# A transformer encoder in one kernel: the order of a gate and up group, and which PSUM pool its accumulators and the attention's transposes use

## The chip, the cores and the metric

The kernel runs on one core of a Trainium2 chip. The metric is device time in microseconds (us), from the first to the last instruction of one launch. The engines named below are TensorE (PE, matrix products, with its weight loads PEld), VectorE (DVE), ScalarE (ACT), GpSimd (POOL) and SyncE (SP, which issues the transfers). Each executes its own list of instructions in the order in which the list was written when the kernel was built.

## The reference

One sequence of 256 tokens with 2048 channels passes two layers and a final norm, all in float32:

```python
h = x + concat(attn, conv, sgu) @ w_out      # all three read RMSNorm(x) @ w_in
x = h + (silu(n @ w_gate) * (n @ w_up)) @ w_down     # n = RMSNorm(h), D_FF = 5632
# attn: 8 query heads on 2 key/value heads of 128, window +-128, a sink logit
#   per head in the softmax, rotary on the first 32 of 128 channels
# conv: GLU, depthwise convolution of width 31, LayerNorm, silu
# sgu:  gelu, LayerNorm of one half, mixing of positions, product with the other half
```

## The kernel before

**Numbers.** The activations are held transposed, as 16 tiles of 128 channels by 256 tokens (`xs`). Every float32 operand is split into a high part and a rest, and each product is three matmuls (xh wh, xh wl, xl wh). Weights are streamed by SP in chunks of 1 MB (`raw`), three at a time. ACT casts half a chunk to its high part (`wh`, L136) and DVE subtracts it (`wl`, L137), four units ahead of PE.

**Stages of a layer.** `proj` (L494) makes the four convolution inputs, two key heads, the values, eight query heads (four pairs p), then the v and u halves of the gating unit. For each query pair: two projections, a copy to `qT` by ACT, the rotary step on DVE (`rope`: a shuffle, two products, a sum, L524 to L529), scores for two token tiles (`pS`, two matmuls each, L536), the softmax on DVE and ACT (scaling and mask L541, maximum L546, exponentials L549, reciprocal L554, scaling L556), and for the pair before, `mix_values` (L561): four transposes of the probabilities into `pT`, a copy `pts` by ACT, the products `po` with the values, and the split of the result into `mix`. The depthwise convolution is 31 steps for each of four channel tiles on DVE (L602), given a low priority so that a scheduler spreads it between other work; its norm (`conv_norm`) is taken up in steps between later work.

**Output projection, then feed-forward.** `feed_sums` (L317) transposes each finished column group of the residual on PE (`pt`, L294), scales it on ACT (`xg`), splits it, and prepares sums and differences (`gf`, `gh`, `gd`). After each group the ACT squares it for the norm (`TokenSums.add`, L346). The feed-forward runs in 11 groups of 512 columns. One group (`gate_up`, L418) walks over eight pairs of 128-channel tiles: a pair of kind P takes eight plain products into the accumulators m2, m3, m4, m5; a pair of kind S takes seven products (a Strassen-like form) into m1 to m7. At its end ACT copies and DVE sums turn the seven accumulators into gate and up.

**PSUM.** There are three pools of buffers: `ps` with tag ps (5), `pm` with tag pm (2) and `pm` with tag pmc (1). All projection accumulators (acc, acct, ao, ad) are in ps. Before, m1, m7, m6, m2, m3 are in ps, m5 in pmc, m4 in pm, and pS, pT, po, pt share pm.

**Order.** The program is written in the order above. A scheduler with a model of the engines then decides the place of each instruction on its engine; a pool gives a buffer to its users in the order of the program, and a later user waits until the earlier one has been read. The chip executes the result without any further choice.

Of the kernel before, what the change touches and what calls it, by code (L numbers as in the profile page):

```python
# [10 lines left out]
F32 = mybir.dt.float32  # L11
# [6 lines left out]
P = 128  # L18
D = 2048
S = 256  # L20
# [19 lines left out]
G = 512  # L40
# [8 lines left out]

UP_PAIRS = [(4, "P"), (5, "S"), (6, "P"), (7, "S"), (0, "P"), (1, "S"), (2, "P"), (3, "P")]  # L50
KIND = dict(UP_PAIRS)
LAST_S = max(i for i, (_, kind) in enumerate(UP_PAIRS) if kind == "S")

PARTS = [(0, 3), (3, 3), (6, 3), (9, 2)]

# [104 lines left out]
def chunk_kinds():  # L160
    kinds = []
    for _ in range(DEPTH):
        kinds += ["P"] * (MIX_COLS * KT // CH + D * KT // CH)
        for _, gn in PARTS:
            kinds += [kind for _, kind in UP_PAIRS] * gn
            kinds += ["P"] * (4 * gn * D // CH)
    return kinds

# [2 lines left out]
def encoder_kernel(  # L171
# [19 lines left out]
    ps = ctx.enter_context(tc.tile_pool(name="ps", bufs=5, space=PSUM))  # L191
# [223 lines left out]
        c = slice(t * P, (t + 1) * P)  # L415
        return xs_part(k, 0)[:, c], xs_part(k, 1)[:, c]

    def gate_up(forms, pending):  # L418

        plan = []
        for i, kind in UP_PAIRS:
            if kind == "S":
                order = [
                    (1, x_form(2 * i, 0)), (2, x_form(2 * i + 1, 0)), (3, forms[i][3]),  # L430
                    (7, forms[i][2]), (5, forms[i][0]), (6, forms[i][1]),
                    (4, x_form(2 * i + 1, 1)),
                ]
                plan.append([(m, x, 0) for m, x in order])
            else:
                one = []
                for j in range(2):
                    x1, x2 = x_form(2 * i + j, 0), x_form(2 * i + j, 1)
                    one += [(2, x1, 0), (3, forms[i][j], 1), (5, x2, 2), (4, x2, 3)]
                plan.append(one)  # L440
        seq = [m for block in plan for m, _, _ in block]
        left = {m: seq.count(m) for m in set(seq)}
        bank = {}
        for m in (1, 7, 6, 2, 3):
            bank[m] = ps.tile([P, G], F32, tag="ps", name=f"m{m}")
        bank[5] = pm.tile([P, G], F32, tag="pmc", name="m5", bufs=1)
        bank[4] = pm.tile([P, G], F32, tag="pm", name="m4", bufs=2)
        begun = set()

        def product(m, x, wh, wl):  # L450
            left[m] -= 1
            three_tok(bank[m], x[0], x[1], wh, wl, m not in begun, left[m] == 0)
            begun.add(m)

        s1, u2, u3 = unit("s1")[:, :G], unit("u2")[:, :G], unit("u3")[:, :G]
        for b, block in enumerate(plan):
            if b == 1 and pending:
                hidden_parts(*pending)
            if UP_PAIRS[b][1] == "S":
                for m, x, _ in block:  # L460
                    product(m, x, *W.take(G))
            else:
                for j in range(2):
                    gh, gl = W.take(G)
                    uh, ul = W.take(G)
                    for m, x, q in block[4 * j:4 * j + 4]:
                        if q in (0, 3):
                            product(m, x, gh, gl)
                        else:
                            product(m, x, uh, ul)  # L470
            if b == LAST_S:
                nc.scalar.copy(out=s1, in_=bank[1])
                nc.vector.tensor_tensor(out=u2, in0=bank[6], in1=s1, op=ALU.add)
                nc.vector.tensor_tensor(out=u3, in0=bank[7], in1=u2, op=ALU.add)
        s3, c22 = unit("s3")[:, :G], unit("c22")[:, :G]
        nc.vector.tensor_tensor(out=s1, in0=bank[2], in1=s1, op=ALU.add)
        nc.scalar.copy(out=s3, in_=bank[3])
        nc.vector.tensor_tensor(out=s3, in0=bank[5], in1=s3, op=ALU.add)
        sub(c22, bank[5], u3)
        nc.vector.tensor_tensor(out=u3, in0=bank[4], in1=u3, op=ALU.add)  # L480
        sub(s3, s3, u2)
        return (s1, u3), (s3, c22)
# [77 lines left out]

    def mix_values(p, t, sm, v):  # L561
        g = p // 2
        pT = pm.tile([P, 4, P], F32, tag="pm", name="pT")
        for hh in range(2):
            for kt in range(2):
                nc.tensor.transpose(
                    pT[:, 2 * hh + kt, :], sm[:, hh, kt * P:(kt + 1) * P], ident
                )
        pts = unit("pts")[:, :4 * P].rearrange("p (a b) -> p a b", a=4)
        nc.scalar.copy(out=pts, in_=pT)  # L570
        po = pm.tile([P, 4, P], F32, tag="pm", name="po")
        for hh in range(2):
            for kt in range(2):
                nc.tensor.matmul(
                    po[:, hh, :], v[:, kt, g * P:(g + 1) * P], pts[:, 2 * hh + kt, :],
                    start=(kt == 0), stop=(kt == 1),
                )
        hilo(
            hm[p][:, :, t * P:(t + 1) * P], hm[p][:, :, S + t * P:S + (t + 1) * P], po[:, :2, :]
        )  # L580
# [103 lines left out]
    sums = Sums("in", nc.gpsimd)  # L684
# [6 lines left out]
    for l in range(DEPTH):  # L691
# [81 lines left out]
        for n, kts, begin, end, complete in OUT_ORDER:  # L773
            if begin:
                accs[n] = token_acc("ao")
            for i, k in enumerate(kts):
                wh, wl = W.take(G)
                token_products(
                    [accs[n]], lambda p: hm_part(k, p), wh, wl,
                    begin == 1 and i == 0, end == 1 and i == len(kts) - 1,  # L780
                )
            if end:
                add_residual(n, accs.pop(n))
            next(cnorm, None)
            if complete:
                feed_sums(n, C_G2 + l * KT, forms)
                sums.add(n)


        rf = sums.rstd(f"b{l}")  # L790
        last_layer = l == DEPTH - 1
        if last_layer:
            gf = consts.tile([P, D], F32, tag="lr", name="gf")
            nc.sync.dma_start(gf, lrow[DEPTH])
        sums = TokenSums(f"n{l}")
        pending = None

        def hidden_parts(ht, i0):
# [4 lines left out]

        for g0, gn in PARTS:
            for j in range(gn):
                gate, up = gate_up(forms, pending)
                if j == 0:
                    new_hm(2 * gn, f"h{l}_{g0}_")
                for t in range(2):
                    nc.scalar.activation(gate[t], gate[t], AF.Silu, scale=rf[:, t:t + 1])  # L810
                    nc.vector.scalar_tensor_tensor(
                        out=up[t], in0=up[t], scalar=rf[:, t:t + 1], in1=gate[t],
                        op0=ALU.mult, op1=ALU.mult,
                    )
                ht = up
                pending = (ht, 4 * j)
            end = g0 + gn == FF // G
            for n in range(NG):
                acc = token_acc("ad")
                for i in range(4 * gn):  # L820
                    if n == 0 and i == 4 * (gn - 1):
                        hidden_parts(*pending)
                        pending = None
                    wh, wl = W.take(G)
                    token_products(
                        [acc], lambda p: hm_part(i, p), wh, wl, i == 0, i == 4 * gn - 1
                    )
                add_residual(n, acc)
                if end:
                    sums.add(n)  # L830
                    if not last_layer:
                        feed_group(n, C_G1 + (l + 1) * KT)
                    elif n < NG - 1:
                        f = slice(n * G, (n + 1) * G)
                        for t in range(2):
                            nc.vector.tensor_tensor(
                                out=xt[t][:, f], in0=xt[t][:, f], in1=gf[:, f], op=ALU.mult
                            )
# [22 lines left out]
def _pack_weights(w_in, w_out, w_gate, w_up, w_down):  # L861
# [17 lines left out]
    for l in range(DEPTH):  # L879
# [18 lines left out]
        for g0, gn in PARTS:  # L898
            for j in range(g0, g0 + gn):
                c = slice(j * G, (j + 1) * G)  # L900
                gu = np.concatenate([w_gate[l][:, c], w_up[l][:, c]], axis=1)
                for i, kind in UP_PAIRS:
                    pair = (2 * i, 2 * i + 1)
                    if kind == "S":
                        put(gu, pair, G, G)
                        put(gu, pair, 0, G)
                    else:
                        put(gu, pair, 0, 2 * G)
            for n in range(NG):
                put(w_down[l], range(4 * g0, 4 * (g0 + gn)), n * G, G)  # L910
# [67 lines left out]
```

## Time and profile before

| | us |
|---|---|
| median of 3 runs | 2006.45 (2006.19 to 2008.48) |
| the profiled execution | 2005.52, span 2003.7 |
| PE busy | 1972.7 (98%), mean granted clock 0.996 |
| DVE busy | 1560.8 (78%) |
| ACT busy | 1060.5 (53%) |
| POOL busy | 27.8 (1%) |
| transfers | 381 MB, mean 190 GB/s |

The span runs from the first to the last instruction. PE is busy in 98% of it, and the chain of work that ended last consists of PE for 97%. A row of the timeline has its start, its duration, the engine, the line, the operation, out<-in, shapes, the count, and in brackets the idle time before it and what ended it. Matmuls overlap in the pipeline, so the cost of one is the distance between starts. PEclk is the clock that PE was granted, as a share of 2.4 GHz.

### The profile page before, as it was taken

The numbers are of one execution on the slowest core, as the hardware profiler recorded it, in microseconds if no ns is written. First come the engines' busy times: TensorE is split into PE (matmuls) and PEld (weight loads), VectorE is DVE, ScalarE is ACT, GpSimd is POOL, SyncE is SP. The second block draws the span as 40 slices with busy tenths as digits, with TensorE's granted clock in tenths as the row PEclk, the third lists the DMA queues.
The fourth block names the chain that finished last, engine by engine and source line by source line (L and its number), as shares of the span: only waits on it lengthen the run. The fifth ranks groups of instructions, "written<-read, shape, count | busy, mean of one in ns | idle before, by whom it ended". The sixth has DMA issues, their size and how long they took to land.

```text
span 2003.7 us, 25514 instructions
## 1 busy us (share of the span) xinstructions
PE 1972.7 (98%) x9998; PEld 1682.5 (84%) x9998; DVE 1560.8 (78%) x1984; ACT 1060.5 (53%) x1367; POOL 27.8 (1%) x49
## 2 busy tenths in 40 slices
PE   8999999999999999999999999999999999999997
PEld 8998887888888888888899888788888888888886
DVE  8997679866886788578679975898678857885784
ACT  6456556544554455445543565656445545554553
POOL 3000000000000000000000000000000000000000
PEclk9999999999999999999999999999999999999999
DMA  7554544555555455545555445355555655555552
GB/s 288 193 187 148 210 162 179 192 214 184 191 201 210 176 202 214 191 184 215 184 176 183 155 145 204 128 210 190 210 184 196 224 192 172 212 205 189 197 203 105
DMA packets 55705, 380.96 MB, mean 190 GB/s; under 512 B 6304, under 2 KB 8608, under 8 KB 10272
## 3 DMA queue, kind: packets, MB, share of 16 engines
q1 hardware_dynamic: 55584, 379.33, 52.5%
q8 instruction: 78, 1.28, 0.3%
q14 instruction: 43, 0.35, 0.0%
HBM read 377.21 MB, written 2.10 MB: 189 GB/s over the span
## 4 chain that ended last, share of the span: by engine, by line
PE 97%; ACT 1%; DVE 1%; DMA 0%; issue 0%; SPq 0%; POOLq 0%; DVEq 0%
PE m L410 15%; PE m L411 15%; PE m L412 15%; PE ad L411 8%; PE ad L412 8%; PE ad L410 8%; PE acc L394 4%; PE acc L395 4%; PE acc L396 4%; PE ao L410 3%; PE ao L411 3%; PE ao L412 3%; PE pt L294 1%; PE acct L514 1%; PE acct L515 1%; PE acct L516 1%
## 5 line engine op out<-in xcount | busy, mean ns | idle before, releaser
L136 ACT CAST wh<-raw 128x1024 fp32r<-128x1024 f32 (+1 forms) x706 | 700.3, 1009 | 693.2 <-PE ad L412 243.5
L137 DVE TENSOR_TENSOR wl<-raw,wh 128x1024 fp32r<-128x1024 f32 (+1 forms) x706 | 817.0, 1169 | 312.6 <-ACT wh L136 309.5
L411 PE MATMUL m<-wl,xs 128*128 128x512 f32 x858 | 335.6, 391 | 0.0
L412 PE MATMUL m<-wh,xs 128*128 128x512 f32 x858 | 333.3, 391 | 0.0
L410 PE MATMUL m<-wh,xs 128*128 128x512 f32 x858 | 310.4, 392 | 7.0 <-ACT xg L317 7.0
L411 PE MATMUL ad<-wl,h 128*128 128x512 f32 x704 | 274.3, 390 | 0.0
L410 PE MATMUL ad<-wh,h 128*128 128x512 f32 x704 | 274.1, 391 | 0.0
L412 PE MATMUL ad<-wh,h 128*128 128x512 f32 x704 | 271.9, 389 | 0.0
L136 ACT CAST wh<-fs 128x1024 fp32r<-128x1024 f32 x132 | 138.9, 1053 | 160.1 <-PE m L412 133.8
L394 PE MATMUL acc<-xs,wh 128*128 128x256 f32 x704 | 196.6, 287 | 7.1 <-ACT xs L283 7.1
L395 PE MATMUL acc<-xs,wh 128*128 128x256 f32 x704 | 200.1, 286 | 0.0
L396 PE MATMUL acc<-xs,wl 128*128 128x256 f32 x704 | 199.5, 286 | 0.0
L137 DVE TENSOR_TENSOR wl<-fs,wh 128x1024 fp32r<-128x1024 f32 x132 | 160.0, 1221 | 47.3 <-ACT wh L136 47.1
L410 PEld LDWEIGHTS m<-wh,xs 128*128 128x128 f32 x858 | 162.2, 189 | 40.4 <-ACT xg L317 7.5
L412 PEld LDWEIGHTS m<-wh,xs 128*128 128x128 f32 x858 | 162.1, 189 | 33.9
L411 PEld LDWEIGHTS m<-wl,xs 128*128 128x128 f32 x858 | 162.0, 189 | 33.8
L412 PEld LDWEIGHTS ad<-wh,h 128*128 128x128 f32 x704 | 132.2, 188 | 27.4
L410 PEld LDWEIGHTS ad<-wh,h 128*128 128x128 f32 x704 | 132.2, 188 | 27.2
L411 PEld LDWEIGHTS ad<-wl,h 128*128 128x128 f32 x704 | 132.2, 188 | 27.0
L394 PEld LDWEIGHTS acc<-xs,wh 128*128 128x128 f32 x704 | 134.2, 194 | 7.7 <-ACT xs L283 7.4
L395 PEld LDWEIGHTS acc<-xs,wh 128*128 128x128 f32 x704 | 136.3, 194 | 0.3
L396 PEld LDWEIGHTS acc<-xs,wl 128*128 128x128 f32 x704 | 136.0, 194 | 0.2
(179 smaller groups left out, 2635.3 us busy)
## 6 DMA issues: line engine op xcount, KB each, us to landing
raw<-w SPq DMA_DIRECT2D x349, 1024.0 KB, 4.8
x<-xT SPq DMA_DIRECT2D x16, 128.0 KB, 4.6
raw<-w SPq DMA_DIRECT2D x4, 512.0 KB, 6.5
lr<-lrow SPq DMA_DIRECT2D x2, 1024.0 KB, 5.0
xt<-xN SPq DMA_DIRECT2D x2, 1024.0 KB, 5.6
out<-xt SPq DMA_DIRECT2D x2, 640.0 KB, 4.4
raw<-w SPq DMA_DIRECT2D x4, 256.0 KB, 4.2
gf<-lrow SPq DMA_DIRECT2D x1, 1024.0 KB, 6.3
```

What stands on the lines that cost most here:

```text
L136: self.nc.scalar.copy(out=h[:, c], in_=r[:, c])
L137: self.nc.vector.tensor_tensor(out=lo[:, c], in0=r[:, c], in1=h[:, c].bitcast(F32), op=ALU.subtract)
L294: nc.tensor.transpose(pt[:, i, t * P:(t + 1) * P], src[t][:, (i0 + i) * P:(i0 + i + 1) * P], ident,)
L394: nc.tensor.matmul(acc, wh, xh, start=first, stop=False)
L395: nc.tensor.matmul(acc, wh, xl, start=False, stop=False)
L396: nc.tensor.matmul(acc, wl, xh, start=False, stop=last)
L410: nc.tensor.matmul(a, xh, wh, start=first, stop=False)
L411: nc.tensor.matmul(a, xh, wl, start=False, stop=False)
L412: nc.tensor.matmul(a, xl, wh, start=False, stop=last)
L514: nc.tensor.matmul(a, xh, wh, start=(k == 0), stop=False)
L515: nc.tensor.matmul(a, xh, wl, start=False, stop=False)
L516: nc.tensor.matmul(a, xl, wh, start=False, stop=(k == KT - 1))
```

## The change

1. The first of the 11 groups of a layer walks over its pairs in the order 4, 6, 5, 7, 0, 1, 2, 3 (P, P, S, S, P, S, P, P) instead of 4, 5, 6, 7, 0, 1, 2, 3 (P, S, P, S, P, S, P, P). The weights are packed in that order.
2. In every group, m2, m3, m5, m4, m1 take buffers of ps, m7 that of pmc and m6 one of pm.
3. `pT`, the transposed probabilities, moves from pm to ps.
4. The eight squares of the feed-forward's norm are no longer issued after each column group, but after block 4 of the first group, and the norm's factor `rf` after that group.

```diff
+UP_FIRST = [(i, KIND[i]) for i in (4, 6, 5, 7, 0, 1, 2, 3)]
...
-    def gate_up(forms, pending):
+    def gate_up(pairs, forms, pending, later=None):
...
-        for m in (1, 7, 6, 2, 3):
+        for m in (2, 3, 5, 4, 1):
             bank[m] = ps.tile([P, G], F32, tag="ps", name=f"m{m}")
-        bank[5] = pm.tile([P, G], F32, tag="pmc", name="m5", bufs=1)
-        bank[4] = pm.tile([P, G], F32, tag="pm", name="m4", bufs=2)
+        bank[7] = pm.tile([P, G], F32, tag="pmc", name="m7", bufs=1)
+        bank[6] = pm.tile([P, G], F32, tag="pm", name="m6", bufs=2)
...
+            if b == 4 and later:
+                later()
...
     def mix_values(p, t, sm, v):
         g = p // 2
-        pT = pm.tile([P, 4, P], F32, tag="pm", name="pT")
+        pT = ps.tile([P, 4, P], F32, tag="ps", name="pT")
...
             if complete:
                 feed_sums(n, C_G2 + l * KT, forms)
+        def ffn_squares(sums=sums):
+            for n in (2, 3, 0, 1):
                 sums.add(n)
-        rf = sums.rstd(f"b{l}")
...
-                gate, up = gate_up(forms, pending)
+                if g0 + j == 0:
+                    gate, up = gate_up(UP_FIRST, forms, pending, ffn_squares)
+                    rf = fsums.rstd(f"b{l}")
+                else:
+                    gate, up = gate_up(UP_PAIRS, forms, pending)
```

The change moves instructions on all engines. First PE in layer 0, where the second projection of the second query pair (acc0_1376) ends; acc0_1502 and acc0_1562 belong to the third pair, pS_1283 and pS_1298 are the scores of the first pair. Before:

```order
L395 MATMUL acc0_1376<-xs7_102,wh31_1247 128x256
L396 MATMUL acc0_1376<-xs7_102,wl31_1248 128x256
L394 MATMUL acc0_1502<-xs0_95,wh32_1317 128x256
L395 MATMUL acc0_1502<-xs0_95,wh32_1317 128x256
...
L394 MATMUL acc0_1562<-xs0_95,wh34_1377 128x256
L536 MATMUL pS_1283<-kT_910,qT_1157 128x256 x2
L536 MATMUL pS_1298<-kT_910,qT_1157 128x256 x2
L395 MATMUL acc0_1562<-xs0_95,wh34_1377 128x256
```

The left-out rows are 46 further matmuls of acc0_1502. Changed, the same place (the lines of the changed file are a few higher); pS_1441 and pS_1456 are the scores of the second pair, pT_1471 and pT_1485 the transposes of the first:

```order
L397 MATMUL acc0_1376<-xs7_102,wh31_1247 128x256
L398 MATMUL acc0_1376<-xs7_102,wl31_1248 128x256
L541 MATMUL pS_1283<-kT_910,qT_1157 128x256 x2
L541 MATMUL pS_1298<-kT_910,qT_1157 128x256 x2
L541 MATMUL pS_1441<-kT_910,qT_1315 128x256 x2
L541 MATMUL pS_1456<-kT_910,qT_1315 128x256 x2
L571 MATMUL pT_1471<-tb_86,sm_1286 128x128 x4
L571 MATMUL pT_1485<-tb_86,sm_1301 128x128 x2
L396 MATMUL acc0_1502<-xs0_95,wh32_1317 128x256
L397 MATMUL acc0_1502<-xs0_95,wh32_1317 128x256
```

The projection matmuls that stood ahead of pS_1283 now stand behind the scores of both pairs and the transposes of the first.

Next DVE at that place, changed: what stands ahead of the last rotary step of the second query pair (qT_1315, the last row), on which pS_1441 waits. cy0 and cy1 are convolution steps, sm_1286 and sm_1301 belong to the scores of the first pair:

```order
L607 SCALAR_TENSOR_TENSOR cy0_264<-cpad0_260,cs_85,cy0_264 128x256
L546 SCALAR_TENSOR_TENSOR sm_1301<-pS_1298,sc_587,tb_86 128x2x256
L549 COPY sm_1444<-cs_85 128x2
L532 TENSOR_TENSOR sw_1436<-sw_1436,tb_86 32x512
L533 TENSOR_TENSOR qT_1315<-qT_1315,tb_86 32x512
L607 SCALAR_TENSOR_TENSOR cy1_265<-cpad3_263,cs_85,cy1_265 128x256
L607 SCALAR_TENSOR_TENSOR cy0_264<-cpad1_261,cs_85,cy0_264 128x256
L607 SCALAR_TENSOR_TENSOR cy1_265<-cpad2_262,cs_85,cy1_265 128x256
L551 TENSOR_REDUCE nm_1289<-sm_1286 128x2
L607 SCALAR_TENSOR_TENSOR cy0_264<-cpad0_260,cs_85,cy0_264 128x256
L551 TENSOR_REDUCE nm_1304<-sm_1301 128x2
L534 TENSOR_TENSOR qT_1315<-qT_1315,sw_1436 32x512
```

The scores of the first pair are worked on ahead of this step; before, the first of these scalings came directly behind the two rotary products and the second five rows later.

Then PE at the end of the last query projection in layer 0 (acc0_1746), changed; acct0_1897 is the projection for the gating unit that follows, pmean, pc_cv and pb_cv belong to the convolution's norm:

```order
L398 MATMUL acc0_1746<-xs7_102,wl39_1592 128x256
L579 MATMUL po_1664<-pts_1662,v_1036 128x128 x4
L579 MATMUL po_1678<-pts_1676,v_1036 128x128 x4
L571 MATMUL pT_1841<-tb_86,sm_1630 128x128 x4
L571 MATMUL pT_1855<-tb_86,sm_1645 128x128 x4
L620 MATMUL pmean_2452<-csum_901,ones_87 128x256
L541 MATMUL pS_1811<-kT_910,qT_1685 128x256 x2
L541 MATMUL pS_1826<-kT_910,qT_1685 128x256 x2
L579 MATMUL po_1848<-pts_1846,v_1036 128x128 x4
L579 MATMUL po_1862<-pts_1860,v_1036 128x128 x4
L363 MATMUL pc_cv_2577<-ones_87,csq_2456 128x1 x2
L571 MATMUL pT_1869<-tb_86,sm_1814 128x128 x4
L382 MATMUL pb_cv_2688<-tb_86,c1_cv_2582 128x128 x2
L579 MATMUL po_1876<-pts_1874,v_1036 128x128 x4
L571 MATMUL pT_1883<-tb_86,sm_1829 128x128 x2
L519 MATMUL acct0_1897<-wh40_1687,xs0_95 128x512
```

All values of the third query pair, the scores of the fourth and most of its transposes now stand ahead of the gating unit's projection.

Last, PE where the first feed-forward group of layer 0 begins. Before; pt_3073 and pt_3088 are the last transposes of the residual:

```order
L411 MATMUL m5_3119<-wl95_3174,xs6_101 128x512
L412 MATMUL m5_3119<-wh95_3173,xs6_101 128x512
L294 MATMUL pt_3073<-tb_86,xt0_93 128x128
...
L294 MATMUL pt_3088<-tb_86,xt0_93 128x128
...
L410 MATMUL m4_3120<-wh88_2963,xs4_99 128x512
L411 MATMUL m4_3120<-wl88_2964,xs4_99 128x512
L412 MATMUL m4_3120<-wh88_2963,xs4_99 128x512
```

Changed; pt_3078 is the last transpose:

```order
L296 MATMUL pt_3078<-tb_86,xt0_93 128x128
L296 MATMUL pt_3078<-tb_86,xt1_94 128x128
L413 MATMUL m4_3097<-wl95_3158,xs5_100 128x512
L414 MATMUL m4_3097<-wh95_3157,xs5_100 128x512
...
L412 MATMUL m5_3096<-wh101_3229,xs0_95 128x512
L412 MATMUL m4_3097<-wh101_3229,xs0_95 128x512
L412 MATMUL m6_3100<-wh95_3157,gh5_2879 128x512
L413 MATMUL m6_3100<-wl95_3158,gh5_2879 128x512
```

The accumulator in pm, m4 before and m6 now, came directly behind the transposes and now comes 37 matmuls behind them.

## Rows read from the trace of the kernel before

**Rows 1.** The page: busy time, share of the span, instructions of each engine

```profile
PE 1972.7 (98%) x9998; PEld 1682.5 (84%) x9998; DVE 1560.8 (78%) x1984; ACT 1060.5 (53%) x1367; POOL 27.8 (1%) x49
```

**Rows 2.** Waits of PE: waited for, us in total, times, longest

```profile
PE m L410 <- ACT xg L317: 7.0, 2, 3.5
PE po L574 <- ACT pts L570: 2.8, 4, 0.7
PE ao L410 <- ACT vg L643: 1.7, 2, 0.8
PE pT L566 <- DVE mix L253: 0.7, 2, 0.4
```

**Rows 3.** Windows: length, busy (instructions) PE PEld DVE ACT POOL, PEclk, DMA share, GB/s

```profile
190.00:194.00 4.00, 2.30 (x17) 1.69 (x15) 1.89 (x6) 3.40 (x6) 0.00 (x0) 1.00 0.00 0
304.00:308.00 4.00, 3.97 (x10) 3.12 (x11) 3.21 (x6) 3.99 (x10) 0.00 (x0) 0.57 0.00 0
1296.00:1302.00 6.00, 6.00 (x17) 4.74 (x18) 4.72 (x10) 5.96 (x14) 0.86 (x1) 0.59 0.00 0
```

**Rows 4.** Timeline of PE at the start of the first feed-forward group, layer 0

```profile
304.03 0.67 PE L410 MATMUL m<-wh,xs 128*128 128x512 f32 x1 [3.52 <-ACT xg L317]
```

**Rows 5.** Timeline of ACT at the same place

```profile
302.55 0.61 ACT L346 ACTIVATE sq<-xt 128x512 f32<-128x512 f32 x1
...
303.16 0.81 ACT L317 ACTIVATE xg<-pt,cs 128x256 f32<-128x256 f32 x2
```

**Rows 6.** Timeline of PE around the first pair's scores, layer 0

```profile
110.00 1.89 PE L536 MATMUL pS<-kT,qT 128*128 128x256 f32 x8
...
111.85 0.28 PE L396 MATMUL acc<-xs,wl 128*128 128x256 f32 x1
111.97 0.28 PE L394 MATMUL acc<-xs,wh 128*128 128x256 f32 x1
```

**Rows 7.** Timeline of DVE at that place, layer 0, and one row of layer 1

```profile
103.55 0.67 DVE L529 TENSOR_TENSOR qT<-qT,sw 32x512 f32<-32x512 f32 x1
104.15 0.86 DVE L602 SCALAR_TENSOR_TENSOR cy<-cpad,cs,cy 128x256 f32<-128x256 f32 x2
105.28 1.23 DVE L137 TENSOR_TENSOR wl<-raw,wh 128x1024 fp32r<-128x1024 f32 x1 [0.27 <-ACT wh L136]
...
106.83 0.72 DVE L524 STREAM_SHUFFLE sw<-qT 32x512 f32<-32x512 f32 x1
...
110.17 0.67 DVE L527 TENSOR_TENSOR sw<-sw,tb 32x512 f32<-32x512 f32 x1
...
111.37 0.73 DVE L541 SCALAR_TENSOR_TENSOR sm<-pS,sc,tb 128x512 f32<-128x512 f32 x1
...
117.28 0.67 DVE L546 TENSOR_REDUCE nm<-sm 128x2 f32<-128x514 f32 x1
...
1095.35 0.67 DVE L529 TENSOR_TENSOR qT<-qT,sw 32x512 f32<-32x512 f32 x1
```

**Rows 8.** Timeline of ACT in attention, layer 0: softmax, copy, mean

```profile
122.68 0.51 ACT L549 ACTIVATE sm<-sm,nm 128x257 f32<-128x257 f32 x1
...
123.59 0.18 ACT L549 ACTIVATION_READ_ACCUMULATOR sm<-sm,nm 128x1 f32 x1
...
128.81 0.91 ACT L556 ACTIVATE sm<-sm,rd 128x256 f32<-128x256 f32 x2
...
133.55 0.59 ACT L570 COPY pts<-pT 128x512 f32<-128x512 f32 x1
...
187.77 0.38 ACT L617 ACTIVATE mean<-pmean 128x256 f32<-128x256 f32 x1
```

**Rows 9.** Timeline of DVE, layer 0: the mean's subtractions

```profile
189.04 1.42 DVE L620 TENSOR_TENSOR cy<-cy,mean 128x256 f32<-128x256 f32 x4
```

**Rows 10.** Timeline of PE, layer 0: values and transposes of one tile

```profile
183.13 1.05 PE L574 MATMUL po<-pts,v 128*128 128x128 f32 x8
184.02 0.60 PE L566 MATMUL pT<-tb,sm 128*128 128x128 f32 x4
```

More of the change, by code (lines that the diff above doesn't have):

```diff
@@ L51 @@
 KIND = dict(UP_PAIRS)
-LAST_S = max(i for i, (_, kind) in enumerate(UP_PAIRS) if kind == "S")
+UP_FIRST = [(i, KIND[i]) for i in (4, 6, 5, 7, 0, 1, 2, 3)]
 PARTS = [(0, 3), (3, 3), (6, 3), (9, 2)]
@@ L163, in chunk_kinds @@
         kinds += ["P"] * (MIX_COLS * KT // CH + D * KT // CH)
-        for _, gn in PARTS:
-            kinds += [kind for _, kind in UP_PAIRS] * gn
+        for g0, gn in PARTS:
+            for j in range(g0, g0 + gn):
+                kinds += [kind for _, kind in (UP_PAIRS if j else UP_FIRST)]
             kinds += ["P"] * (4 * gn * D // CH)
@@ L416, in x_form @@
         return xs_part(k, 0)[:, c], xs_part(k, 1)[:, c]
-    def gate_up(forms, pending):
+    def gate_up(pairs, forms, pending, later=None):
+        last_s = max(i for i, (_, kind) in enumerate(pairs) if kind == "S")
         plan = []
-        for i, kind in UP_PAIRS:
+        for i, kind in pairs:
             if kind == "S":
@@ L458, in gate_up @@
                 hidden_parts(*pending)
-            if UP_PAIRS[b][1] == "S":
+            if pairs[b][1] == "S":
                 for m, x, _ in block:
@@ L470, in gate_up @@
                             product(m, x, uh, ul)
-            if b == LAST_S:
+            if b == 4 and later:
+                later()
+            if b == last_s:
                 nc.scalar.copy(out=s1, in_=bank[1])
@@ L794, in encoder_kernel @@
             nc.sync.dma_start(gf, lrow[DEPTH])
-        sums = TokenSums(f"n{l}")
+        fsums, sums = sums, TokenSums(f"n{l}")
         pending = None
@@ L901, in _pack_weights @@
                 gu = np.concatenate([w_gate[l][:, c], w_up[l][:, c]], axis=1)
-                for i, kind in UP_PAIRS:
+                for i, kind in UP_PAIRS if j else UP_FIRST:
                     pair = (2 * i, 2 * i + 1)
```

## The prediction

> **What bounds the kernel now.** I read the page first. TensorE (PE) is busy for 1972.7 of the 2003.7 us span [rows 1], so the time is PE's work plus PE's idle time, and every other engine counts only where PE waits for it. The waits of PE come next [rows 2]. Apart from the start of the program they are two kinds. The first matmul of m4 in each layer waits 7.0 us in total for the ScalarE (ACT) line that scales a transposed pair, which is 3.5 us a layer. At the end of attention, po, ao and pT wait 2.8 + 1.7 + 0.7 = 5.2 us, 2.6 a layer. The windows come third, for what an idle time does to the clock [rows 3]: after the 3.5 us wait the granted clock stands at 0.57 over 4 us in layer 0 and at 0.59 over 6 us in layer 1 (full is 2.4 GHz, half is 1.2). That costs 4 x 0.43 = 1.7 us and 6 x 0.41 = 2.5 us more. In the broken stretch 190 to 194, PE works only 2.30 of 4 us and the clock stays at 1.00. So what this kernel could win lies in two places, and everywhere else PE runs without a gap. That includes all of attention up to its end, and that is what the change puts at stake.
>
> **The transition into the gate and up groups (a gain).** Before, eight transposes stand in a row on PE, and the m4 matmul behind them needs the PSUM buffer that the last of them filled. It starts at 304.03 after 3.52 us idle [rows 4]. On ACT two squares stand ahead of the scaling that empties this buffer; the second one starts at 302.55 and the scaling only at 303.16 [rows 5]. The change takes the squares out of that queue, lets four accumulators of the opening pairs (m2, m3, m5, m4) live in the larger pool, and lets m6, which comes into use later, take the buffer that is emptied last. The order shows 37 matmuls between the last of the transposes and the first of m6. By it each 128x512 matmul then finds its inputs, except that m1 waits for one weight cast; I put this at 0.9 us a layer, without a fall of the clock. The gain is 7.0 + 1.7 + 2.5 - 2 x 0.9 = 9.4 us for both layers. Bounds: if a wait as long as the present one remains, nothing comes back beyond the squares' 2 x 1.2 us (say 2); if none remains, 11.2. The eight squares themselves run later beside PE's matmuls, on an ACT that is 53% busy [rows 1]; the norm's factor is first used when the first group ends, three pairs later. I cost them at 0; without that cover they cost one square, 0.6 (303.16 less 302.55), each, 5 us.
>
> **The probabilities' transposes in the larger pool (a loss).** A pool hands out its buffers in program order. In the program, pT of one head pair comes ahead of the projection of a later pair. When pT came from pm, the projection accumulators (acc, acct) never stood behind it, and the order of before runs 49 of the next head's projection matmuls between the end of acc_1376 and the first scores pS, and more than 90 behind those. When pT comes from ps, acc_1502 gets its buffer after the pTs, and the order shows it on PE behind pS of both token tiles and of the next pair and behind six pT. PE executes in order, so nothing fills the time while DVE and ACT work through the softmax. There are two such places in each layer.
>
> *Place A.* Projection matmuls start 0.12 apart and a pS pair costs 1.73 (110.00 to 111.85 less one matmul) [rows 6]. The 49 matmuls that move behind take 5.9 us, so acc_1376 ends at 110.00 - 5.9 = 104.1. The first pS pair runs 104.1 to 105.9, and the next pS needs the last rotation step (TENSOR_TENSOR qT<-qT,sw) of its own query pair. VectorE (DVE) is strictly in order, and up to its row at 104.15 the queue is the same in both kernels. Behind that stand, with the spacings of [rows 7]: 2 convolution steps (0.80, to 104.95), a weight difference that waits for its cast (105.28 to 106.42), 4 convolution steps and a shuffle (4 x 0.40 + 0.63, to 108.65), score scaling and its small copy (0.73, to 109.38), one step, scaling and copy (0.40 + 0.73, to 110.5), two rotation products (1.2, to 111.7), 3 steps, a reduce, a step, a reduce (4 x 0.40 + 2 x 0.60, to 114.5), and the rotation step itself, done at 115.15. PE idles 9.3 us. The second pS pair ends at 116.9. Its pT wait for the reciprocals and the scalings of the first pair (ACT, about 0.45 each [rows 8]): DVE has four more convolution steps ahead of the reciprocal (to 116.8), so six transposes (0.15 each) run 117.4 to 118.6, where acc_1502 starts. From 104.1 to 118.6 are 14.5 us with 2 x 1.73 + 0.9 of work: 10.1 idle. The same walk in layer 1, from its row at 1095.35 [rows 7], lets the second pS start at 1106.7 after 8.8 us idle and gives 9.6. Sum: 19.7 us. A bound below is the wait for the rotation step alone, 9.3 + 8.8 = 18; above, with a late reciprocal, 22.
>
> *Place B.* This is the end of attention, where the last query projection ends (t = 0), and then everything of the last two head pairs is queued before acct, the gating unit's projection. The chain is the softmax of the last tiles and the convolution's norm on two engines, one leg after the other, in durations of [rows 8, 9]. ACT: a weight cast 1.05, the query copy and two mix casts (0.38 each, as the mean row), two pairs of exponentials (1.09 each: 122.68 to 123.77): to 4.5 with a gap. Four scalings 1.82, two pts copies 1.0, the mean 0.38: to 7.8. DVE: four subtractions of the mean 1.42, score scaling 0.73, a sum of squares 0.4 (as one subtraction), reduce 0.6: to 11.0. ACT again: exponential pair 1.09, cast 0.38, square 0.4, single exponential 0.5, two scalings 0.91, exponential 0.5, cast 0.38, copy 0.5, scaling 0.45: to 16.3. Then one po (0.9) and a pT (0.15): acct starts at 17.4. PE's own work inside (8 projection matmuls excluded) is two po, two pT, pmean, a pS pair, two po, pT, po and small ones, with 0.89 for a po and 0.60 for a pT [rows 10]: about 9.4. So 8.0 idle a layer, 16.0 in all. Here I trust each leg less: if the legs on DVE and ACT overlap better, 12; with one leg more, 20. The 5.2 us of waits at the end of attention go, since the last values are then covered by acct matmuls.
>
> *The clock.* An idle time of 3.5 us cost 1.7 and 2.5 us of half clock behind it [rows 3]. A has one of 9 us, B several shorter ones. The nearest rows give about 2 for each of the four places: 8 us. Bounds: 0 (the broken stretch 190 to 194 lost none) and 4 x 2.5 = 10. The Trainium skill, "TensorE: Matmul & The Clock Gate", section "A second HAM failure mode: psum-queue depth-cycling", says that frequent short idles between groups of matmuls make the clock swing between its two levels, so that throughput suffers though each matmul looks normal. The stretch 190 to 194 at 1.00 does not bear it out for this kernel. By that rule the work inside B would run at half clock as well, which is the first half of rival 4.
>
> **The other banks at group boundaries.** In the 20 later groups the exchanged accumulators change which eviction a new group's first matmuls wait for: m3 for the copy of the old m3, m5 and m4 for DVE sums. m2's matmuls come first and cover them; before, no such wait shows in [rows 2], so I take 0. The bound is one 128x512 copy of 0.59 us [rows 8] in each: 12 us. A gain is not possible there, since nothing is lost now. The changed weight order of the first group moves the same bytes and products: 0.
>
> **The sum**, on the profiled execution (2005.5 us; the median of the runs is 0.9 above): 2005.5 + 19.7 + 16.0 - 5.2 + 8 - 9.4 = 2034.6; as a median 2035.5. I say 2035.
>
> **Rivals.**
> 1. *Faster: only the transition counts.* If ACT and DVE, with PE idle, reach the softmax so early that the pT buffers never hold back a projection, A and B vanish and the time is 2005.5 - 9.4, with the attention end gone too 1991. It decides at one point: DVE must deliver the second rotation step by 105.9 instead of 115.15. For it speaks that DVE is 78% busy over the span [rows 1], so it has slack on average; against it that its queue stands full from 103.55 to 117.28 [rows 7], and that PE waits 3.52 us at 304.03 although other matmuls that need nothing are behind the waiting one [rows 4]. "PSUM — Partial Sum Buffer" of the Trainium skill, section "Engine vs sequencer instructions", has both queues strictly in order and matmuls starting and completing in program order; by it this rival stands at its small chance. 6%, near 1994.
> 2. *Slower, without loss of clock.* Both stalls stand, but pS and pT in between keep the clock up as in 190 to 194: 2026.6. 15%, 2022 to 2029.
> 3. *B is hidden.* Legs overlap and the last values finish beside acct, only A stays: 2005.5 + 19.7 + 4 - 5.2 - 9.4 = 2015. 8%, 2010 to 2021.
> 4. *A B at half clock, or boundary waits.* The matmuls on B's chain (po, pS, pT, some 3 us a layer by [rows 6, 10]) take twice as long: 2034.6 + 6 = 2041. Or all 20 boundaries wait for a copy: + 12, 2047. 7% for each.
> 5. *The change does not do what it says*, the transition keeps its wait and the pTs are late anyway: without the 9.4 gain 2044; it shares rival 4's end. 2%. That gains and losses cancel near 2006 has 3%.
>
> **Range and chances.** The forecast, 2029 to 2040, has 52%. The range must reach to rivals 2 and 4 and to part of 3: 2017 to 2047. A measurement of this kernel can tell about 0.2%, 4 us, from no change. Faster 0.06 (rival 1), same 0.03, slower 0.91.
>
> **What would show it.** In the profile after, the waits of PE should be led by pS for the rotation line and by pT for the scalings, with about 9 us as the longest; m for the scaling of the transposed pair should have shrunk from 7.0 to under 2; PE's idle time should have risen from about 31 to about 57 us. Windows near 106 to 119 and near the end of the last query projection should show PE under half busy, and a granted clock near 0.5 behind them. Wrong would be: PE without a gap there (rival 1), or idle there with a clock at 1.00 (rival 2), or new waits of m spread over all groups (rival 4).

## The result, and the profile after

The changed kernel takes 2025.7 us (median of four runs, 2025.27 to 2026.64); the kernel before, on the same chip, 2006.3. The ratio is 1.0099, with an interval of 1.0087 to 1.0110: slower by 19.4 us. The forecast was 2035, in a range of 2017 to 2047, slower.

The page of the kernel after, busy time by engine, answers to [rows 1]:

```profile
PE 1976.8 (98%) x9998; PEld 1685.5 (83%) x9998; DVE 1559.3 (77%) x1984; ACT 1053.9 (52%) x1365; POOL 26.9 (1%) x49
```

PE is busy 4.1 us longer, and the span is 20.1 us longer (2023.8), so 16 us of the loss are idle time of PE, which rises from 31.0 to 47.0 us. The waits of PE (us in total, times, longest) answer to [rows 2]:

```profile
PE pS L541 <- DVE qT L534: 18.4, 3, 8.9
...
PE pT L571 <- ACT sm L561: 3.6, 3, 3.1
PE pmean L620 <- DVE csum L617: 1.9, 1, 1.9
PE m L412 <- ACT wh L137: 1.3, 2, 0.7
PE po L579 <- ACT pts L575: 1.1, 1, 1.1
PE po L579 <- DVE sm L546: 0.5, 1, 0.5
PE pc_cv L363 <- DVE csq L631: 0.5, 1, 0.5
PE pb_cv L382 <- POOL c_cv L375: 0.5, 1, 0.5
```

The 3.5 us wait of m4 is gone, and so are the waits of ao and of pT for `mix` at the end of attention. In their place stand pS for the rotation step, with 8.9 us as the longest, and pT for the scalings. (The third of the pS waits, 0.9 us, is in place B of layer 1.) m still waits 0.65 us a layer for a weight cast.

Windows cut at the ends of places A and B (columns as in [rows 3]: length, PE busy, ..., PEclk, DMA share, GB/s). The first four are of layer 0, the last two are A and B of layer 1:

```profile
104.65:120.34 15.69, 6.67 (x24) 5.20 (x23) 15.42 (x38) 6.39 (x15) 0.65 (x2) 0.67 0.56 199
120.34:148.02 27.68, 27.68 (x229) 27.47 (x228) 26.43 (x54) 14.54 (x28) 0.47 (x6) 1.00 0.34 124
148.02:164.98 16.96, 12.34 (x75) 9.95 (x73) 13.43 (x36) 13.49 (x39) 0.85 (x3) 0.90 0.12 51
164.98:301.76 136.78, 136.78 (x718) 117.60 (x716) 81.66 (x105) 64.55 (x81) 1.98 (x2) 1.00 0.52 185
...
1106.70:1121.26 14.56, 5.89 (x25) 4.60 (x23) 14.56 (x36) 6.39 (x15) 0.00 (x0) 0.77 0.20 72
1148.94:1166.67 17.73, 13.42 (x74) 10.56 (x73) 14.24 (x37) 13.63 (x40) 0.69 (x1) 0.81 0.11 47
```

In layer 0, between A and B and after B, PE never idles and its clock is full. In A it idles 9.0 of 15.7 us, in B 4.6 of 17.0, and the granted clock over these two stretches is 0.67 and 0.90 on average.

The whole of attention and the output projection, from the first projection matmul of a layer to the first matmul of m, both layers, first before:

```profile
5.24:286.06 280.82, 276.18 (x1815) 254.07 (x1815) 230.23 (x384) 152.69 (x245) 21.79 (x30) 1.00 0.56 203
1002.47:1277.79 275.32, 272.62 (x1816) 250.95 (x1814) 215.84 (x367) 142.16 (x218) 2.83 (x4) 1.00 0.49 173
```

and after:

```profile
5.26:301.76 296.50, 280.47 (x1815) 256.67 (x1815) 230.39 (x383) 150.32 (x241) 20.99 (x30) 0.98 0.53 192
1013.25:1303.45 290.20, 277.22 (x1815) 253.63 (x1814) 216.01 (x366) 139.45 (x214) 3.24 (x4) 0.98 0.47 164
```

The two stretches became 30.6 us longer: 21.7 us are idle time of PE and 8.9 us are longer busy time for the same matmuls.

Place A on PE, with the first projection matmul behind it:

```profile
104.89 1.97 PE L541 MATMUL pS<-kT,qT 128*128 128x256 f32 x8
115.79 3.75 PE L541 MATMUL pS<-kT,qT 128*128 128x256 f32 x8 [8.94 <-DVE qT L534]
119.34 1.25 PE L571 MATMUL pT<-tb,sm 128*128 128x128 f32 x6
120.34 0.36 PE L396 MATMUL acc<-xs,wh 128*128 128x256 f32 x1
```

The same place on DVE; the last row is the first reciprocal:

```profile
104.68 0.86 DVE L607 SCALAR_TENSOR_TENSOR cy<-cpad,cs,cy 128x256 f32<-128x256 f32 x2
...
114.98 0.67 DVE L534 TENSOR_TENSOR qT<-qT,sw 32x512 f32<-32x512 f32 x1
...
117.16 0.15 DVE L559 RECIPROCAL rd<-den 128x2 f32<-128x2 f32 x1
```

And the scalings on ACT, for which the transposes wait:

```profile
117.34 1.70 ACT L561 ACTIVATE sm<-sm,rd 128x256 f32<-128x256 f32 x4 [1.16 <-DVE rd L559]
```

The walk of the prediction is found again, 0.5 us later throughout, since the first inputs of this execution came that much later. It put the rotation step's end at 115.15; it ends where the next row begins, 115.58. It put the second pS at 115.2, and it starts at 115.79. What it did not contain: this pS takes 3.55 us (to 119.34), not 1.73, because the clock is at half (1.2 GHz). Not all of that is lost: the last two of the six transposes need the third scaling, which is done at 118.6 (117.34 + 3 x 0.43). At full clock acc_1502 could then have started near 118.9, an estimate from two transposes of 0.15 behind 118.6; it starts at 120.34, some 1.4 us later.

Place B on PE, layer 0; the last row is the start of the gating unit's projection:

```profile
148.03 1.95 PE L579 MATMUL po<-pts,v 128*128 128x128 f32 x16
153.07 1.86 PE L571 MATMUL pT<-tb,sm 128*128 128x128 f32 x8 [3.10 <-ACT sm L561]
...
164.98 0.48 PE L519 MATMUL acct<-wh,xs 128*128 128x512 f32 x1
```

From 148.02 to 164.98 are 16.96 us, where the walk had 17.4; layer 1 has 17.7.

### The profile page after: what moved, and what is told of

Same layout as the page of the kernel before. It is cut to its first block, busy times and chain, and to the rows that moved or that the text cites. A ratio compares the mean times of both kernels' runs of the same rounds, so it can differ in the third digit from the quotient of the medians.

```text
span 2023.8 us, 25513 instructions
## 1 busy us (share of the span) xinstructions
PE 1976.8 (98%) x9998; PEld 1685.5 (83%) x9998; DVE 1559.3 (77%) x1984; ACT 1053.9 (52%) x1365; POOL 26.9 (1%) x49
## 4 chain that ended last, share of the span: by engine, by line
PE 96%; DVE 2%; ACT 1%; DMA 0%; issue 0%; SPq 0%; POOLq 0%; POOL 0%; DVEq 0%; ACTq 0%
PE m L414 15%; PE m L413 15%; PE m L412 15%; PE ad L414 8%; PE ad L412 8%; PE ad L413 8%; PE acc L396 4%; PE acc L397 4%; PE acc L398 4%; PE ao L413 3%; PE ao L412 3%; PE ao L414 3%; PE pt L296 1%; PE acct L520 1%; PE acct L521 1%; PE acct L519 1%
```

## The experiments

Times are medians; the kernel before was at 2006.1 to 2006.3 beside them.

**1. pT back.** The changed kernel with

```diff
-        pT = ps.tile([P, 4, P], F32, tag="ps", name="pT")
+        pT = pm.tile([P, 4, P], F32, tag="pm", name="pT")
```

> The changed kernel with pT back in pm, the other three parts kept. Theory (pT in ps alone makes both attention stalls; the transition gains its 8.5 us by itself): the waits of pS for the rotation step vanish, the 5.2 us of waits at the end of attention come back, time near 2006.3 - 8.5 = 1998. Rival (other accumulator banks cost something at the 20 group boundaries that the changed kernel hides in the sum): above 2002, with waits of m spread over the groups. Rival (stalls come from the order or the banks as well): pS waits stay, above 2015.

Measured: 1994.96 us, ratio to before 0.9944 (0.9929 to 0.9959), 3 us under the theory's 1998. Its waits of PE apart from the start:

```profile
PE po L579 <- ACT pts L575: 2.8, 4, 0.7
PE ao L412 <- ACT vg L648: 1.7, 2, 0.8
PE m L412 <- ACT wh L137: 1.3, 2, 0.7
PE pT L571 <- DVE mix L255: 0.7, 2, 0.4
```

No pS waits, the end of attention waits as in [rows 2], and m waits for a cast 0.65 us a layer. One line makes the difference between 11 us faster and 19 us slower.

**2. pT alone.** The kernel before with that line the other way.

> The kernel before with only pT moved to ps. Theory: both attention stalls in full, 28 us over two layers net of the 5.2 at the end of attention, the 7.0 us wait of m4 and its half clock stay: 2006.3 + 28 = 2034. Rival (the stalls need the other parts): under 2020.

Measured: 2036.59 us, ratio 1.0153 (1.0136 to 1.0170). Its waits:

```profile
PE pS L536 <- DVE qT L529: 17.4, 3, 8.9
PE m L410 <- ACT xg L317: 7.1, 2, 3.5
...
PE pT L566 <- ACT sm L556: 6.7, 3, 3.1
```

It costs 30.5 us here and 30.7 us in the changed kernel (2025.7 - 1994.96): the loss belongs to this part and adds to the others. The transition's wait is untouched.

**3. The squares alone.** The kernel before with

```diff
+            if b == 4 and later:
+                later()
...
+        def ffn_squares(sums=sums):
+            for n in (2, 3, 0, 1):
                 sums.add(n)
...
-        rf = sums.rstd(f"b{l}")
...
+                    gate, up = gate_up(forms, pending, ffn_squares)
+                    rf = fsums.rstd(f"b{l}")
```

so that the squares stand behind block 4 and the norm's factor behind the first group.

> The kernel before with only the eight squares moved behind block 4 of the first group. Theory (the squares are only a part of the queue ahead of the scaling): the wait of m4 shrinks by two squares, 3.5 to about 2.3 a layer, part of the half clock goes with it: 2006.3 - 2.4 to - 6, near 2002. Rival (the two squares are the whole matter): 1998. Rival (squares only shift the wait): 2006.

Measured: 2007.81 us, ratio 1.0009 (1.0000 to 1.0019): no gain, which fits the third guess. But the wait did shrink as the theory said, from 7.0 to 4.6:

```profile
PE m L410 <- ACT xg L317: 4.6, 2, 2.3
...
PE m L410 <- ACT wh L136: 1.9, 3, 0.9
...
PE m L411 <- DVE wl L137: 1.3, 3, 0.5
```

Two windows of layer 0 (columns as before), and the two waits on PE between them:

```profile
304.00:308.00 4.00, 4.00 (x19) 3.30 (x18) 3.43 (x6) 4.00 (x11) 0.00 (x0) 1.00 0.00 0
...
312.00:316.00 4.00, 4.00 (x11) 2.75 (x10) 3.96 (x5) 4.00 (x11) 0.00 (x0) 0.57 0.16 66
```

```profile
310.18 0.73 PE L410 MATMUL m<-wh,gh 128*128 128x512 f32 x2 [0.94 <-ACT wh L136]
311.44 0.50 PE L411 MATMUL m<-wl,gh 128*128 128x512 f32 x1 [0.52 <-DVE wl L137]
```

PE waits 1.2 us a layer less for the scaling (2.3 against 3.5), and then waits further on, in an S pair, for the cast and the difference of its weights. All waits of m together are 7.8 us, where they were 7.0. The clock, which had stayed at 1.00 after the 2.3 us wait, falls after these shorter ones. The gain was turned into a later wait. The theory of this run was wrong about the time.

**4. The banks alone.** The kernel before with

```diff
-        for m in (1, 7, 6, 2, 3):
+        for m in (2, 3, 5, 4, 1):
...
-        bank[5] = pm.tile([P, G], F32, tag="pmc", name="m5", bufs=1)
-        bank[4] = pm.tile([P, G], F32, tag="pm", name="m4", bufs=2)
+        bank[7] = pm.tile([P, G], F32, tag="pmc", name="m7", bufs=1)
+        bank[6] = pm.tile([P, G], F32, tag="pm", name="m6", bufs=2)
```

> The kernel before with only the accumulators' pools exchanged (m2, m3, m5, m4, m1 in ps, m7 in pmc, m6 in pm). Theory (what waits is the user of the last pm buffer, and m6 now comes late): the 7.0 us wait of m goes, and with it the half clock: near 1999. Rival (m7 and m6 of the first S pair take m4's place as the waiting matmul): 2004 to 2006. Rival (group boundaries): new waits of m in all groups, above 2006.

Measured: 1992.84 us, ratio 0.9934 (0.9919 to 0.9949). All its waits of PE:

```profile
PE acc L394 <- ACT xs L283: 6.8, 2, 5.3
PE po L574 <- ACT pts L570: 2.8, 4, 0.7
PE ao L410 <- ACT vg L643: 1.7, 2, 0.8
PE pT L566 <- DVE mix L253: 0.7, 2, 0.4
```

No wait of m is left, in the first group or in the other ten. This part alone brings 13.2 us, more than the three parts together in run 1, and more than the 7 that the theory of this run and the 11.2 that the prediction's bound had for it. Where the last 2 us come from is not shown.

**5 and 6. Banks with the squares moved, and banks with the new order of pairs.** The diffs are those of run 4 with run 3, and run 4 with the list UP_FIRST.

> The kernel before with the banks exchanged and the squares moved, order of pairs and pT as before. Theory (the banks bring the whole 13 us; the 2 us that the changed kernel with pT back is behind come from the squares, which now stand among the weight casts on ACT that PE needs for its S pairs): 1995, with a wait of m for the cast wh of 0.5 to 1 a layer. Rival (the 2 us come from the order of the pairs): 1993, without such a wait.

> The kernel before with the banks exchanged and the order of the first group's pairs changed, squares and pT as before. Theory (the order neither gains nor loses): 1993. Rival (two S pairs next to each other make PE wait for their casts, whatever the squares do): 1995, with the wait of m for wh of 0.65 a layer.

Measured: 1993.05 us (0.9936, 0.9921 to 0.9951) and 1992.92 us (0.9936, 0.9920 to 0.9953), neither with a wait of m. The theory of run 5, that the squares cost 2 us, is out, and so is run 6's rival. So neither part costs anything with the banks, and neither brings anything. The 2 us by which run 1 lies behind come only where both are there; 1.3 of them are the wait for the cast in its list. Why only then was not settled.

**7. Place A without place B.** The changed kernel with

```diff
-        pT = ps.tile([P, 4, P], F32, tag="ps", name="pT")
+        pool, tag = (ps, "ps") if p < 2 else (pm, "pm")
+        pT = pool.tile([P, 4, P], F32, tag=tag, name="pT")
```

> The changed kernel with pT in ps for the first two head pairs of a layer and in pm for the last two. Theory (each pT in ps bars the accumulators allocated after it, and nothing else): place A stands as it is, some 11 us a layer; place B vanishes, and so do the waits at the end of attention, because the late start has let DVE and ACT catch up: 1995 + 22.3 - 5.4 = 2012. Rival (A and B are one shortage of DVE, so what A doesn't wait is waited later anyway): B's waits appear in another form, 2020 to 2026.

Measured: 2009.26 us, ratio 1.0017 (1.0008 to 1.0026), near the theory's 2012. Of its waits:

```profile
PE pS L541 <- DVE qT L534: 17.5, 2, 8.9
...
PE m L412 <- ACT wh L137: 1.3, 2, 0.7
```

A stands, B and the waits at the end of attention are gone. So A costs 2009.3 - 1995.0 + 5.2 = 19.5 us (the 5.2 are the waits that this kernel also saves), and B 2025.7 - 2009.3 = 16.4.

**8. A short convolution.** The changed kernel with 8 steps for each channel tile:

```diff
-        for t in range(TAPS):
+        for t in range(8):
```

> The changed kernel with 8 instead of 31 convolution steps for each channel tile (the convolution's result is not the reference's). Theory (the size of A is the length of DVE's queue ahead of the rotation step, 5 of its 9 us convolution steps, and PE now has some 20 projection matmuls as cover): no wait of pS for the rotation step over 4 us, pT waits for the scalings of about 3 us a layer, B shorter by the convolution's norm which is done earlier; 2025.7 - 2 x 7 = 2012, between 2006 and 2016. Rival (the wait is the latency of the softmax chain itself, whatever DVE has to do): 2020 or more.

Measured: 2023.12 us, ratio 1.0086 (1.0071 to 1.0102). The theory gave 2012, the rival 2020 or more, and the rival's number holds. Its two longest waits, and a window behind its place A in layer 0:

```profile
PE pT L571 <- ACT sm L561: 12.1, 5, 4.9
PE pS L541 <- DVE qT L534: 9.3, 2, 4.7
```

```profile
114.00:120.00 6.00, 6.00 (x28) 5.61 (x28) 1.56 (x4) 0.42 (x1) 0.00 (x0) 0.60 0.47 176
```

The rotation step no longer holds PE in A: the longest wait is 4.9 us for the scalings, about half of what it was. But then come 6 us of full work at a clock of 0.60. With 8 steps of convolution the wait in A is the latency of the softmax, and the half clock falls on work that could have run at full speed. The two waits of pS for the rotation step, 4.7 us each, are now in place B (at 154.03 in layer 0), which the theory had forecast shorter. So the length of DVE's queue set much of the size of A in the changed kernel, and it is not the reason that A is there; the schedule of this kernel differs in other places too.

**9 and 10. The clock's own price.** Run 7's kernel with a seed (an ACT copy of scores, so that the added work stands behind the first scores) and 34 matmuls without use, and a twin with one:

```diff
+        if p == 0 and t == 1:
+            seed = unit("seed", F32R)[:, :P]
+            nc.scalar.copy(out=seed, in_=pS[:, 0, :P])
+            idle = pm.tile([P, G], F32, tag="pmc", name="idle", bufs=1)
+            with tc.high_priority(offset=-300):
+                for i in range(34):
+                    nc.tensor.matmul(idle, seed, xs[0], start=True, stop=True)
```

> The kernel of the run with pT in ps for the first two pairs alone, with 34 matmuls of 128x512 without use (0.23 us each, 7.7 in all) that PE can do in the wait of place A, behind the first pair's scores. Theory (half clock behind the wait costs time of its own): the granted clock stays at 1.00 in A, the second scores take 1.7 instead of 3.6 us, and the time is 4 to 6 us under that of its twin with one such matmul. Rival (what the clock loses falls into time in which PE waits for ACT's scalings anyway): within 1.5 us of the twin.

> The twin of the run before it: one useless matmul instead of 34, the same place in the program. Both theories: place A as in the kernel with pT in ps for the first two pairs, half clock behind a wait of 9 us, near 2009 (2007 to 2012).

Measured: 2011.5 us (2009.6 to 2013.8; ratio to before 1.0028, 1.0017 to 1.0039) and 2012.97 us (2012.6 to 2014.0; 1.0035, 1.0021 to 1.0048). In layer 0 the schedule put four of the transposes ahead of the second pS in both, so that A's wait is here one of pT for the scalings (10.0 us in the twin). Place A of layer 0, from the end of the projection to the start of acc_1502, and a window of layer 1, first with 34:

```profile
104.06:119.65 15.59, 12.66 (x58) 9.83 (x57) 15.32 (x38) 7.52 (x18) 2.28 (x2) 1.00 0.37 135
...
1112.00:1116.00 4.00, 4.00 (x17) 3.57 (x16) 3.72 (x10) 0.53 (x2) 0.00 (x0) 0.57 0.00 0
```

and with one, A and a window inside it:

```profile
104.51:121.28 16.77, 6.36 (x25) 4.72 (x24) 16.50 (x41) 7.62 (x18) 3.46 (x2) 0.69 0.33 125
...
112.00:116.00 4.00, 0.00 (x0) 0.00 (x0) 4.00 (x9) 2.19 (x8) 0.00 (x0) 0.50 0.00 0
```

In layer 0 the clock stays at 1.00 in the one and falls to half in the other, and A is 1.2 us shorter where it stays. In layer 1 the added matmuls did not keep it up: behind a wait of 2.1 us for the scalings it is 0.57 from 1112 to 1116, in which PE works without a gap. So the medians, which differ by 1.5 us with ranges that overlap, compare one place with a kept clock and not two. The theory, 4 to 6 us, is out. The rival holds: where the clock was kept up, it was worth 1.2 us of A.

**11. A version that beats both.** The kernel before with the banks of run 4, six `sm` buffers, pT as in run 7, and

```diff
-            now = [(p, t, scores(l, p, t, qT, kT, sc), v) for t in range(2)]
-            for args in before:
-                mix_values(*args)
-            before = now
+            if p == 3:
+                for args in before.pop(0):
+                    mix_values(*args)
+            before.append([(p, t, scores(l, p, t, qT, kT, sc), v) for t in range(2)])
...
-        for args in before:
-            mix_values(*args)
         va = proj_tok(512)
+        for one in before:
+            for args in one:
+                mix_values(*args)
```

> The kernel before with the banks exchanged, and the probabilities' part of the first pair moved behind the projections of the fourth, that of the others behind the gating unit's v projection; pT in ps for the first two pairs, in pm for the others (six sm buffers). Theory (a pT in ps costs only what it comes too late for the next accumulator): with 100 and 70 projection matmuls more as cover there are at most waits of 1 to 3 us a layer, and the 5.2 us at the end of attention go: 1987 to 1993. Rival (DVE is late by more than that cover): waits of pT for the scalings over 5 us a layer, 1998 or more.

Measured: 1988.23 us, ratio 0.9911 (0.9894 to 0.9927), the fastest kernel of the study, 4.6 us under run 4. Its only wait of PE apart from the start:

```profile
PE pT L567 <- ACT sm L556: 3.0, 2, 1.7
```

The same buffers in ps, taken by a later place in the program: now the accumulators that come behind them find the probabilities nearly ready. The banks bring 13.2 of the 17.9 us (run 4). For the other 4.6, the 5.2 us of waits at the end of attention are gone and 3.0 us of pT are new; what else is in it, and what part the six `sm` buffers and the two pools of pT have, was not tried by itself.

## Why the prediction was right, and which term was not

- **The mechanism and the sign: shown.** pT in ps puts accumulators behind the softmax; this one part costs 30.5 us alone and 30.7 with the others (runs 1, 2).
- **Place A, forecast 19.7 us: measured 19.5** (run 7). The end of the rotation step was 0.1 us off once the late start is taken out. By the windows A is longer than the walk, 15.69 us where it had 14.5, and 14.56 where layer 1's 9.6 idle and 4.36 of work make 14.0; so some 2 us were saved elsewhere in run 7, and that the two numbers agree so closely is in part luck.
- **Place B, forecast 16.0 us: measured 16.4** (the changed kernel less run 7). Its length, 16.96 and 17.73 us, is near the walk's 17.4. (The walk's last leg on ACT adds up to 5.1 us, which ends at 16.1 and not at 16.3; that changes nothing.)
- **The end of attention, forecast 5.2 us saved:** the waits of ao and of pT for `mix` are absent from the changed kernel's list; one of po for `pts`, 1.1 us, is left inside B of layer 1.
- **The transition, forecast 9.4 us gained.** From the first m to the first projection of the next layer, 716.41 us became 711.49; from the first m of layer 1 to the last matmul of the program, 714.18 became 708.54. That is 4.9 + 5.6 = 10.6, inside the bounds. The wait for the cast that I put at 0.9 was 0.65 a layer.
- **The clock, forecast 8 us on top: the term that was mis-sized.** Attention with the output projection became 30.6 us longer. The forecast's terms for it are 19.7 + 16.0 - 5.2 = 30.5 without the clock, and 38.5 with it. The clock did fall to half, but inside A and B and not, as forecast, behind them: the windows that follow them in layer 0 stand at 1.00. There my walks had booked as idle the time in which PE waits for the scalings and the next leg, and PE's slow matmuls ran partly in just that time: A idles 9.0 us where the walk had 10.1, B 4.6 where it had 8.0, and over both layers the idle time grew by 21.7 us and not by 30.5, while busy time grew by 8.9. I added nearly the same microseconds a second time. What the clock did cost shows in A: about 1.2 us in layer 0, by which A is longer than its walk and by which it was shorter with the clock kept up (run 9), and at most 0.6 us in layer 1 by the walk. For B this was not tried by itself; that its length is the walk's leaves little room for it. The sign "idle time from about 31 to about 57 us" failed with this term: it came to 47.0.
- **What the prediction did not see:** which part makes the transition's gain. It named the squares' place in ACT's queue, m4's move and the late m6 together. The banks do it alone (run 4), and the squares alone do nothing for the time (run 3).
- **The rivals.** The second, both stalls without a cost of the clock, 2026.6, is what came (2025.7, below the 2029 to 2040 that had the largest chance), though for another reason than it gave: the clock fell, and cost little. The third (B hidden, 2015) and the fourth (waits at the group boundaries) are out: B stands, and no such wait shows in the changed kernel or in run 4. The first was out by the walk: the rotation step came at 115.58, not before 106. On the rule of "PSUM — Partial Sum Buffer" in the Trainium skill, section "Engine vs sequencer instructions" (matmuls start in program order), the trace agrees: PE executes nothing between the end of the first pS (106.86) and the second (115.79), and acc_1502, which stands behind, starts at 120.34. On the rule of "TensorE: Matmul & The Clock Gate" in the Trainium skill, section "A second HAM failure mode: psum-queue depth-cycling": part of B did run at the lower level (0.90 on average in layer 0, 0.81 in layer 1), as that rule has it, but the 2041 that I worked out for a B at half clock did not come.

## What to carry to other kernels

A PSUM tile that needs a long chain on other engines must not be handed out, in program order, ahead of accumulators of the same pool that have work ready; look at the in-order list of the busiest engine for what now stands behind it, and either keep such tiles in a pool of their own or move their place in the program until the chain is done when their turn comes. When a stall is put together from a walk, a lower clock inside it is no further cost so long as the next input is later still; add it only for work that nothing else holds up (in A that was about 1.2 us; in run 8 it fell on the projections behind A). Before moving work out of a queue, try the buffer that the waiting matmul needs: here exchanging two accumulators for two others between pools brought the whole gain, and moving the queue's work brought nothing.

## What the runs showed of the hardware that was not expected

- A single wait of 2.3 us left the granted clock at 1.00, and two waits of 0.94 and 0.52 us that came 7 us behind it were followed by a clock of 0.57 over 4 us (run 3); in the kernel before, one wait of 3.5 us was followed by 0.57 over 4 us too [rows 3]. The price of an idle time can't be read from its own length alone.
- The clock can fall while PE waits, before the next matmul: in run 10, the twin, it stands at 0.50 in a window of layer 0 in which PE executes nothing (112 to 116).
